# High and low weight parts in alternating places: stationary tiles read with a step of two elements, at eight offsets in turn

## The chip, the cores and the metric

The kernel runs on one core of a Trainium2 chip. Its time is the device time of one execution in microseconds (us); lower is better. Five engines work side by side: PE (matmul; the profile lists its loads of stationary tiles apart, as PEld), DVE (vector), ACT (scalar), POOL, and SP, which issues the DMAs.

## What is computed

One layer of a streaming encoder on 256 tokens of width 2048, all in float32: a mixer of two branches (multi-scale retention and gated DeltaNet), cross-attention to 256 memory tokens, and an MLP of hidden width 8192. Cut to what matters here:

```python
def reference(x, mem, positions, ...):
    h = rms_norm(x, norm_mix_g)
    x = x + hybrid_mixer(h, positions, w_in, conv_w, ..., w_out)   # w_in: 2048 x 18464
    h = rms_norm(x, norm_x_g)
    mem_n = rms_norm(mem, norm_mem_g)
    x = x + cross_attention(h, mem_n, w_xq, w_xkv, w_xo)
    h = rms_norm(x, norm_ffn_g)
    x = x + jnp.square(jax.nn.relu(h @ w_ff1)) @ w_ff2
    return rms_norm(x, norm_final_g)
```

Nearly all of the work is the products of the 256 tokens with the weight matrices, some 390 MB of weights read once.

## The kernel before

A float32 product is made of three products in float32r, a rounded form that PE streams at one pass: every operand is split into a high part (rounded) and a low part (what is left), and high x high, high x low and low x high are added in PSUM.

`fetch` brings a piece of weights to SBUF: one DMA of 1 MB into `raw` (L96), then for each of two halves of 128x1024 a copy on ACT that rounds (L106, writes `whi`) and a subtraction on DVE (L107, writes `wlo`). `whi` and `wlo` are separate tiles with three buffers each, so ACT and DVE run up to three halves ahead of PE. The activations lie in quads: four blocks of 128 features, each with 256 tokens of high parts and 256 of low parts side by side (`both`).

There are two kinds of products:

- `blocks` makes feature-major results (features on the partitions, tokens along them). The weights are the stationary tile, the activations move. For each k-tile and each of two output blocks, L187 multiplies the high weights with the high and the low activations at once (512 columns), L188 the low weights with the high activations (256 columns). One fetch serves 8 k-tiles of two blocks, 16 such pairs. `blocks` makes the delta rule's q, k and v, the retention's q and k, the keys of the cross-attention, w_out, w_xq, w_xo, and the first layer of the MLP. Its evacuation adds the two parts (L194 on ACT, L195 on DVE).
- `chunk` makes token-major results. The activations are the stationary tile, the weights move with 512 columns: L147, L148, L149 for the three products, 16 k-tiles and two token halves to a chunk. It makes the gates, the values and the second layer of the MLP.

The MLP alternates: for each of four parts of the hidden width, a stage of 8 `blocks` (first layer; `evac_h` squares and splits the hidden values into the quads `hid` by L973, L975, L976) and a stage of 4 `chunk`s (second layer).

Where the tiles lie in SBUF: `blocks` puts `whi` 56 elements after the start of its tile and `wlo` at 0 (`AT_BLOCKS`), `chunk` both at 0; pad tiles (`PAD1`, `PAD2`) shift the quads. The order of the instructions on each engine comes from a scheduler that simulates a timeline; fetches have high priority.

Of the kernel before, what the change touches and what calls it, by code (L numbers as in the profile page):

```python
# [11 lines left out]
F32R = mybir.dt.float32r  # L12
# [5 lines left out]
P = 128  # L18
D = 2048
S = 256  # L20
# [10 lines left out]
THETA = 10000.0  # L31


AT_BLOCKS = (56, 0)
PAD1, PAD2 = 8, 80
TWO_PI = 2.0 * math.pi
BIG = 1.0e30
# [14 lines left out]
def trunk(ctx: ExitStack, tc: tile.TileContext, x, mem, positions, norm_mix_g, w_in, conv_w, gdn_a_log, gdn_dt_bias,  # L52
# [8 lines left out]
    wp = ctx.enter_context(tc.tile_pool(name="wpipe", bufs=3))  # L61
    hqp = ctx.enter_context(tc.tile_pool(name="hq", bufs=1))
# [4 lines left out]
    def stream_ps():  # L67
        s0 = psp.tile([P, 512], F32, name="s0", tag="s0", bufs=2)
        s1 = psp.tile([P, 512], F32, name="s1", tag="s1", bufs=2)
        return s0, s1  # L70

    def bank():
        return psp.tile([P, 512], F32, name="b", tag="b", bufs=4)
# [4 lines left out]
    def step():  # L78
        if steps and next(steps[0], steps) is steps:
            steps.pop(0)  # L80
# [3 lines left out]
            step()  # L84


    def fetch(pieces, k, n, rush=False, hold=None, at=(0, 0)):


        raw = wp.tile([P, k * n], F32, name="raw", tag="raw", bufs=3)  # L90
        rv = raw.rearrange("p (k n) -> p k n", k=k)
        with tc.high_priority(offset=100000):
            for off, ap in pieces:
                src = ap.rearrange("(k p) n -> p k n", p=P)
                for ks in ((slice(0, k // 2), slice(k // 2, k)) if rush else (slice(0, k),)):
                    nc.sync.dma_start(rv[:, ks, off:off + ap.shape[1]], src[:, ks, :])  # L96
            got = []
            for i in range(2):
                if hold:
                    both = hold().both  # L100
                    hi, lo = (both[:, a:a + 2, :].rearrange("p a s -> p (a s)") for a in (0, 2))
                else:
                    hi, lo = (wp.tile([P, k * n // 2 + room], F32R, name=nm, tag=nm, bufs=3)[:, a:a + k * n // 2]
                              for nm, a, room in zip(("whi", "wlo"), at, (64, 0)))
                src = raw[:, i * k * n // 2:(i + 1) * k * n // 2]
                act.activation(hi, src, AF.Copy)  # L106
                vec.tensor_sub(lo, src, hi.bitcast(F32))  # L107
                got.append((hi.rearrange("p (k n) -> p k n", n=n), lo.rearrange("p (k n) -> p k n", n=n)))
        return got

    def split(dst, src, at=slice(None)):
        h, l = (a[:, at] for a in dst)
        act.activation(h, src, AF.Copy)
        vec.tensor_sub(l, src, h.bitcast(F32))
# [6 lines left out]
    class Quad(tuple):  # L121
        pass

    def new_quad(pl, bufs):
        both = pl.tile([P, 4, 2 * S], F32R, name="q", tag="q", bufs=bufs)
        quad = Quad((both[:, :, 0:S], both[:, :, S:2 * S]))
        quad.both = both
        return quad

    def quad_a():  # L130
        return new_quad(hqp, 5)

    def chunk(quads, pieces_of, evac, before=None, hold=None):


        ps = stream_ps()
        parts = [(t, 0, 512, ps[t]) for t in range(NT)]
        if hold:
            parts[1:] = [(1, 0, 256, ps[1][:, :256]), (1, 256, 512, bank()[:, :256])]
        held = {q: fetch(pieces_of(q), 4, 512, hold=hold) for q in ((2, 3) if hold else ())}  # L140

        def products(q, i, part, halves):
            t, c0, c1, o = part
            xh, xl = (a[:, i, t * P:(t + 1) * P] for a in quads[q])
            wh, wl = (a[:, i % 2, c0:c1] for a in halves[i // 2])
            first, last = q == 0 and i == 0, q == 3 and i == 3
            pe.matmul(o, xh, wh, start=first, stop=False)  # L147
            pe.matmul(o, xh, wl, start=False, stop=False)  # L148
            pe.matmul(o, xl, wh, start=False, stop=last)  # L149

        for q in range(4):
            if q not in held:
                if before:
                    before(q)
                halves = fetch(pieces_of(q), 4, 512, rush=before is not None and q == 0)
                for i in range(4):
                    for part in parts:
                        products(q, i, part, halves)
                    if i % 2:
                        step()  # L160
        for part in parts:
            for q, halves in held.items():
                for i in range(4):
                    products(q, i, part, halves)
            with tc.high_priority(offset=50000):
                evac(part[0], part[3], part[1], part[2])
# [4 lines left out]
    def blocks(quads, w, c0, nb, evac):  # L171

        k = 16 // nb
        ps = stream_ps()
        n = nb * P
        for g in range(KT // k):
            halves = fetch([(0, w[g * k * P:(g + 1) * k * P, c0:c0 + n])], k, n, at=AT_BLOCKS)
            for i in range(k):  # L180
                kk = g * k + i
                xh, xhl = quads[kk // 4][0][:, kk % 4, :], quads[kk // 4].both[:, kk % 4, :]
                wh, wl = halves[i // (k // 2)]
                for b in range(nb):
                    bs = slice(b * P, (b + 1) * P)
                    lh, ll = wh[:, i % (k // 2), bs], wl[:, i % (k // 2), bs]
                    pe.matmul(ps[b], lh, xhl, start=kk == 0, stop=False)  # L187
                    pe.matmul(ps[b][:, :S], ll, xh, start=False, stop=kk == KT - 1)  # L188
                if i % (k // 2) == k // 2 - 1:
                    step()  # L190
        for b in range(nb):
            with tc.high_priority(offset=50000):
                o = sm.tile([P, S], F32, name="bo", tag="bo", bufs=2)
                act.activation(o, ps[b][:, S:], AF.Copy)  # L194
                vec.tensor_add(o, o, ps[b][:, :S])  # L195
                evac(b, o)
# [108 lines left out]
    def values(n):  # L305
        vo = kv.tile([P, NT, 512], F32, name="vo", tag="vo", bufs=2)

        def evac_kv(t, ps, c0, c1):
            if not mem_scale:
                for c in range(4):  # L310
                    row_squares(mem_rows[c], ssqm, c)
                mem_scale.append(rms_cols("nm", ssqm))
            act.activation(vo[:, t, :], ps, AF.Copy, scale=mem_scale[0][:, t:t + 1])

        chunk(memq, cols(w_xkv[0], D + n * 512), evac_kv, before=load_mem if n == 0 else None)
        nc.sync.dma_start(vv_d[:, :, n * 512:(n + 1) * 512], vo)

    values(0)
    load_gains(16, (norm_mix_g, norm_x_g, norm_ffn_g))
    h1 = [quad_a() for _ in range(4)]  # L320
    ssq1 = cp.tile([P, NT, 4], F32, name="ssq1")
    xcs = [load_rows(c, x, 0) for c in range(4)]
# [5 lines left out]
    for k2 in range(8):  # L328
# [10 lines left out]
        for f in range(2):  # L339
            k = 2 * k2 + f  # L340
# [160 lines left out]

    values(2)
    blocks(h1, w_in[0], C_GA, 1, decay_rows)
    values(3)
    for h in range(4):
# [213 lines left out]
    def retention(j, yr):  # L719
# [16 lines left out]
        def evac_v(t, ps, c0, c1):  # L736
            split(v, ps, t)

        chunk(h1, cols(w_in[0], C_RV + 512 * j), evac_v)
        gng = mx.tile([P, 512], F32, name="gng", tag="g_sq", bufs=1)  # L740
        nc.sync.dma_start(gng, ret_gn_g[0, 512 * j:512 * j + 512].partition_broadcast(P))
# [70 lines left out]
    def take_back(q):  # L812
        if q:
            back = quad_a()
            act.activation(back[0], kept[q - 1], AF.Copy)
            vec.tensor_sub(back[1], kept[q - 1], back[0].bitcast(F32))
            merged.append(back)

    gate_retention, gate_delta_rule = gates()
    for j in range(5):  # L820
# [3 lines left out]
        if j:  # L824
            if j < 4:
                quad = mx.tile([P, 4, S], F32, name="mg", tag="mg", bufs=3)
                kept.append(quad)
            else:
                finish_steps()
                quad = quad_a()  # L830
# [21 lines left out]
    def quad_b():  # L852
        return new_quad(q2p, 4)
# [49 lines left out]
    for h in range(XH):  # L903
# [31 lines left out]
        quad = quad_a()  # L935
        for d2 in range(2):
            ops = bank()
            ov = ops.rearrange("p (d s) -> p d s", d=2)
            for d in range(2):
                c0 = (2 * d2 + d) * P  # L940
# [24 lines left out]
    for fb in range(4):  # L965
        hid = []
        for b2 in range(8):
            hs = fp.tile([P, 2, S], F32, name="hs", tag="hs", bufs=2)
            if b2 % 2 == 0:
                hid.append(quad_a())  # L970

            def evac_h(b, ps):
                vec.scalar_tensor_tensor(hs[:, b, :], ps, 0.0, ps, op0=ALU.max, op1=ALU.mult)  # L973
                qh, ql = (a[:, b2 % 2 * 2 + b, :] for a in hid[-1])
                act.activation(qh, hs[:, b, :], AF.Copy)  # L975
                vec.tensor_sub(ql, hs[:, b, :], qh.bitcast(F32))  # L976

            blocks(h3, w_ff1[0], fb * D + b2 * 256, 2, evac_h)
        for n in range(4):
# [13 lines left out]
            def evac_last(t, ps, c0, c1):  # L993
# [20 lines left out]
                for c in (0, 3, 1, 2):  # L1014
# [13 lines left out]
                  hold=quad_b if last else None)  # L1028
# [27 lines left out]
```

## Time and profile before

| | us |
|---|---|
| median of 3 runs (2107.12 to 2109.13) | 2108.48 |
| the profiled execution | 2106.88 |
| its span, first to last instruction | 2105.2 |
| PE busy (share of the span) | 2083.3 (99%) |
| PE's loads busy | 1796.9 (85%) |
| DVE busy | 1407.7 (67%) |
| ACT busy | 1091.6 (52%) |

The profile shows one execution. A row of a group names the line, the engine, the operation and the tiles (written <- read; for a matmul the moving operand comes first, then the stationary one), the number of instructions, then busy time and the mean of one in ns, then the idle time of the engine ahead of them and what ended it. Matmuls are pipelined: the duration of one holds a latency, so what one costs in a row of many is the distance of two starts. In a window's row stand, after the stretch and its length, each engine's busy time with its count of instructions, the granted PE clock and the share and rate of the DMA engines.

### The profile page before, as it was taken

Reading aid. Unit: us, or ns where it says so; the run is one execution under the profiler, and the core shown is the slowest. Engines: PE = TensorE matmul, PEld = TensorE weight load, DVE = VectorE, ACT = ScalarE, POOL = GpSimd, SP = SyncE. Lnnn points to the kernel's source line nnn. Section 1 sums busy time; section 2 is a strip of 40 time slices with the busy share of each in tenths; the row PEclk is TensorE's granted clock in tenths of the full one; section 3 lists DMA queues with packets and bytes.
Section 4 is the critical chain, followed back from the end, with each engine's and each line's share of the span. In section 5 each row is a group of like instructions: output and inputs, shape, how many; then the busy total and the mean of one; then the engine's idle time right before and its main releaser. Section 6 shows DMA issues by size and latency. Waiting matters only on the chain.

```text
span 2105.2 us, 28781 instructions
## 1 busy us (share of the span) xinstructions
PE 2083.3 (99%) x11172; PEld 1796.9 (85%) x11172; DVE 1407.7 (67%) x2225; ACT 1091.6 (52%) x1700; POOL 28.7 (1%) x39
## 2 busy tenths in 40 slices
PE   8999999999999999999999999999999999999998
PEld 6878888888888888888888899888888888888887
DVE  6756779678758884878557666766556555645655
ACT  7565564565446454655355555554434434434444
POOL 0000000000000000000000000000000000000000
PEclk9999999999999999999999999999999999999999
DMA  8778655555545555555458654566566556556653
GB/s 298 243 242 258 201 181 193 176 171 182 184 156 193 192 175 166 182 183 190 153 174 256 202 186 155 180 197 186 199 190 191 197 187 197 188 192 198 185 198 140
DMA packets 316010, 405.91 MB, mean 193 GB/s; under 512 B 16593, under 2 KB 224481, under 8 KB 315745
## 3 DMA queue, kind: packets, MB, share of 16 engines
q1 hardware_dynamic: 315872, 404.08, 59.5%
q8 instruction: 87, 1.43, 0.3%
q14 instruction: 51, 0.41, 0.1%
HBM read 390.40 MB, written 13.65 MB: 192 GB/s over the span
## 4 chain that ended last, share of the span: by engine, by line
PE 93%; DMA 3%; ACT 2%; DVE 1%; SPq 1%; issue 0%; ACTq 0%; POOLq 0%; POOL 0%; DVEq 0%
PE s L187 32%; PE s L188 17%; PE s L148 13%; PE s L149 13%; PE s L147 13%; PE b L675 2%; DMA dec_d<-dec_w 1%; ACT whi L106 1%; DVE wlo L107 1%; ACT dec_w L493 1%; PE b L581 1%; DMA xc<-x 1%; PE b L117 0%; DMA xt_d<-xt 0%; PE b L119 0%; PE b L118 0%
## 5 line engine op out<-in xcount | busy, mean ns | idle before, releaser
L107 DVE TENSOR_TENSOR wlo<-raw,whi 128x1024 fp32r<-128x1024 f32 x702 | 858.3, 1223 | 522.0 <-ACT whi L106 516.2
L106 ACT ACTIVATE whi<-raw 128x1024 fp32r<-128x1024 f32 x702 | 742.3, 1059 | 730.9 <-PE s L149 387.0
L187 PE MATMUL s<-q,whi 128*128 128x512 f32 x3088 | 1063.4, 390 | 0.7 <-ACT whi L106 0.4
L188 PE MATMUL s<-q,wlo 128*128 128x256 f32 x3088 | 845.3, 281 | 5.2 <-DVE wlo L107 5.1
L187 PEld LDWEIGHTS s<-q,whi 128*128 128x128 f32 x3088 | 570.8, 188 | 111.5 <-ACT whi L106 1.6
L188 PEld LDWEIGHTS s<-q,wlo 128*128 128x128 f32 x3088 | 579.0, 188 | 20.1 <-DVE wlo L107 8.8
L148 PE MATMUL s<-wlo,q 128*128 128x512 f32 x1264 | 495.6, 392 | 1.0 <-DVE wlo L107 1.0
L149 PE MATMUL s<-whi,q 128*128 128x512 f32 x1264 | 492.4, 390 | 0.0
L147 PE MATMUL s<-whi,q 128*128 128x512 f32 x1264 | 454.1, 391 | 0.0
L148 PEld LDWEIGHTS s<-wlo,q 128*128 128x128 f32 x1264 | 238.0, 188 | 50.1 <-DVE wlo L107 2.5
L147 PEld LDWEIGHTS s<-whi,q 128*128 128x128 f32 x1264 | 237.5, 188 | 49.2 <-ACT q L249 0.4
L149 PEld LDWEIGHTS s<-whi,q 128*128 128x128 f32 x1264 | 237.6, 188 | 48.0
L194 ACT ACTIVATE bo<-s 128x256 f32<-128x256 f32 x193 | 73.1, 379 | 118.8 <-PE s L188 105.9
L195 DVE TENSOR_TENSOR bo<-bo,s 128x256 f32<-128x256 f32 x193 | 80.4, 417 | 44.4 <-ACT bo L194 44.1
L534 DVE SCALAR_TENSOR_TENSOR acc<-bo,cw,acc 128x255 f32<-128x255 f32 (+2 forms) x144 | 66.8, 480 | 1.5
L636 DVE TENSOR_TENSOR pr<-lw,tw 32x31 f32<-32x31 f32 (+15 forms) x124 | 40.4, 325 | 8.4 <-DMA lw<-scr_l 6.5
L638 DVE TENSOR_TENSOR tw<-tw,pr 32x31 f32<-32x31 f32 (+15 forms) x124 | 40.5, 327 | 2.1
L782 ACT ACTIVATE gth<-s 128x512 f32<-128x512 f32 x32 | 18.9, 591 | 22.5 <-PE s L149 18.3
L984 DVE SCALAR_TENSOR_TENSOR res<-s,rstd3q,res 128x512 f32<-128x512 f32 (+1 forms) x32 | 22.3, 735 | 11.8 <-PE s L149 11.8
L973 DVE SCALAR_TENSOR_TENSOR hs<-bo 128x256 f32<-128x256 f32 x64 | 27.0, 422 | 1.1
L976 DVE TENSOR_TENSOR q<-hs,q 128x256 fp32r<-128x256 f32 x64 | 26.8, 419 | 0.8 <-ACT q L975 0.8
L531 ACT ACTIVATE acc<-bo,cw 128x256 f32<-128x256 f32 x48 | 24.1, 503 | 4.5 <-DVE bo L195 4.4
(292 smaller groups left out, 1084.3 us busy)
## 6 DMA issues: line engine op xcount, KB each, us to landing
raw<-w_in SPq DMA_DIRECT2D x144, 1024.0 KB, 5.1
raw<-w_ff SPq DMA_DIRECT2D x128, 1024.0 KB, 5.4
raw<-w_xkv SPq DMA_DIRECT2D x31, 1024.0 KB, 5.9
raw<-w_out SPq DMA_DIRECT2D x16, 1024.0 KB, 5.7
raw<-w_xq SPq DMA_DIRECT2D x16, 1024.0 KB, 6.5
raw<-w_xo SPq DMA_DIRECT2D x16, 1024.0 KB, 5.5
dec_d<-dec_w SPq DMA_DIRECT2D x16, 192.0 KB, 4.0
dec<-dec_d SPq DMA_DIRECT2D x8, 384.0 KB, 3.2
```

What stands on the lines that cost most here:

```text
L106: act.activation(hi, src, AF.Copy)
L107: vec.tensor_sub(lo, src, hi.bitcast(F32))
L147: pe.matmul(o, xh, wh, start=first, stop=False)
L148: pe.matmul(o, xh, wl, start=False, stop=False)
L149: pe.matmul(o, xl, wh, start=False, stop=last)
L187: pe.matmul(ps[b], lh, xhl, start=kk == 0, stop=False)
L188: pe.matmul(ps[b][:, :S], ll, xh, start=False, stop=kk == KT - 1)
L194: act.activation(o, ps[b][:, S:], AF.Copy)
L195: vec.tensor_add(o, o, ps[b][:, :S])
L534: vec.scalar_tensor_tensor(acc[:, d:], ps[:, :S - d], cw[:, j, blk:blk + 1], acc[:, d:], op0=ALU.mult, op1=ALU.add)
L638: vec.tensor_sub(tw[:, j + 1:32, 0:j + 1], tw[:, j + 1:32, 0:j + 1], pv)
L675: pe.matmul(pv[:, i, :], lhs(i), rhs[:, i, :], start=True, stop=True)
```

## The change

The high and the low part of a half of weights now share one tile `w`. For `blocks` (`mixed=True`) they alternate, element by element: high parts at even, low parts at odd places. So a stationary tile of 128 columns is read with a step of two elements (8 bytes), and ACT and DVE write, and DVE reads, with that step. For `chunk` the high parts fill the first half of the tile and the low parts the second, contiguous as before. The hidden values of the MLP (`hid`, the second layer's stationary operand) alternate in the same way; all other quads stay as they were. The place in the tile where the parts begin is no longer fixed: every call of `blocks` or `chunk` takes the next of eight offsets, 0 to 56 elements, in steps of 8 (32 bytes).

```diff
-AT_BLOCKS = (56, 0)
+AT_WEIGHTS = (0, 8, 16, 24, 32, 40, 48, 56)
...
-    def fetch(pieces, k, n, rush=False, hold=None, at=(0, 0)):
+    def fetch(pieces, k, n, rush=False, hold=None, at=0, mixed=False):
...
+            half = k * n // 2
             for i in range(2):
+                src = raw[:, i * half:(i + 1) * half]
...
-                    hi, lo = (wp.tile([P, k * n // 2 + room], F32R, name=nm, tag=nm, bufs=3)[:, a:a + k * n // 2]
-                              for nm, a, room in zip(("whi", "wlo"), at, (64, 0)))
-                src = raw[:, i * k * n // 2:(i + 1) * k * n // 2]
+                    w = wp.tile([P, 2 * half + 64], F32R, name="w", tag="w", bufs=3)[:, at:at + 2 * half]
+                    w = w.rearrange("p (n e) -> p e n" if mixed else "p (e n) -> p e n", e=2)
+                    hi, lo = w[:, 0], w[:, 1]
...
+    def next_at():
+        used.append(0)
+        return AT_WEIGHTS[len(used) % len(AT_WEIGHTS)]
...
+    def sides(both, mixed):
+        return both.rearrange("p f (s e) -> p f e s" if mixed else "p f (e s) -> p f e s", e=2)
+
+    def new_quad(pl, bufs, mixed=False):
         both = pl.tile([P, 4, 2 * S], F32R, name="q", tag="q", bufs=bufs)
-        quad = Quad((both[:, :, 0:S], both[:, :, S:2 * S]))
-        quad.both = both
+        pair = sides(both, mixed)
+        quad = Quad((pair[:, :, 0], pair[:, :, 1]))
+        quad.both, quad.pair = both, pair
         return quad
...
     def chunk(quads, pieces_of, evac, before=None, hold=None):
...
+        at = next_at()
...
-                halves = fetch(pieces_of(q), 4, 512, rush=before is not None and q == 0)
+                halves = fetch(pieces_of(q), 4, 512, rush=before is not None and q == 0, at=at)
...
     def blocks(quads, w, c0, nb, evac):
...
+        at = next_at()
         for g in range(KT // k):
-            halves = fetch([(0, w[g * k * P:(g + 1) * k * P, c0:c0 + n])], k, n, at=AT_BLOCKS)
+            halves = fetch([(0, w[g * k * P:(g + 1) * k * P, c0:c0 + n])], k, n, at=at, mixed=True)
...
-                xh, xhl = quads[kk // 4][0][:, kk % 4, :], quads[kk // 4].both[:, kk % 4, :]
+                xh, xhl = quads[kk // 4][0][:, kk % 4, :], quads[kk // 4].pair[:, kk % 4]
...
-                hid.append(quad_a())
+                hid.append(quad_a(mixed=True))
```

After the change the lines are numbered anew: the copy and the subtraction of `fetch` are L108 and L109 (before L106, L107), the products of `blocks` L202 and L203 (L187, L188), those of `chunk` L161 to L163 (L147 to L149), the writes of the hidden quads L990 and L991 (L975, L976).

More of the change, by code (lines that the diff above doesn't have):

```diff
@@ L109, in fetch @@
         return got
+    used = []
+    def next_at():
+        used.append(0)
+        return AT_WEIGHTS[len(used) % len(AT_WEIGHTS)]
     def split(dst, src, at=slice(None)):
@@ L122, in trunk, with quad_a @@
         pass
-    def new_quad(pl, bufs):
+    def sides(both, mixed):
+        return both.rearrange("p f (s e) -> p f e s" if mixed else "p f (e s) -> p f e s", e=2)
+    def new_quad(pl, bufs, mixed=False):
         both = pl.tile([P, 4, 2 * S], F32R, name="q", tag="q", bufs=bufs)
-        quad = Quad((both[:, :, 0:S], both[:, :, S:2 * S]))
-        quad.both = both
-        return quad
-    def quad_a():
-        return new_quad(hqp, 5)
+        pair = sides(both, mixed)
+        quad = Quad((pair[:, :, 0], pair[:, :, 1]))
+        quad.both, quad.pair = both, pair
+        return quad
+    def quad_a(mixed=False):
+        return new_quad(hqp, 5, mixed)
     def chunk(quads, pieces_of, evac, before=None, hold=None):
```

## The prediction

> **What bounds the kernel now.** I read the page first (engines, chain, costliest groups), then the waits of PE, then single stages by windows, and last the starts of single matmuls in the timeline.
>
> ```profile
> span 2105.2 us, 28781 instructions
> PE 2083.3 (99%) x11172; PEld 1796.9 (85%) x11172; DVE 1407.7 (67%) x2225; ACT 1091.6 (52%) x1700; POOL 28.7 (1%) x39
> ...
> PEclk9999999999999999999999999999999999999999
> ...
> PE 93%; DMA 3%; ACT 2%; DVE 1%; SPq 1%; issue 0%; ACTq 0%; POOLq 0%; POOL 0%; DVEq 0%
> PE s L187 32%; PE s L188 17%; PE s L148 13%; PE s L149 13%; PE s L147 13%; PE b L675 2%; DMA dec_d<-dec_w 1%; ACT whi L106 1%; DVE wlo L107 1%; ACT dec_w L493 1%; PE b L581 1%; DMA xc<-x 1%; PE b L117 0%; DMA xt_d<-xt 0%; PE b L119 0%; PE b L118 0%
> ```
>
> PE is busy all through, at the full granted clock, and five matmul lines make 88% of the chain. PE busy is not PE at its peak, so the question is how far apart its matmuls start. Does PE wait for anybody?
>
> ```profile
> PE s L188 <- DVE wlo L107: 5.1, 7, 1.6
> PE b L236 <- DMA xc<-mem: 4.6, 1, 4.6
> ...
> PEld s L188 <- DVE wlo L107: 8.8, 10, 2.0
> ```
>
> Hardly: the largest entries are 5.1 us in 2105. So the change can only matter through the time from one matmul's start to the next, or by making somebody late who is in time today. The starts, in a first-layer stage of the MLP (blocks) and, by count, in a second-layer stage (chunk), where the window's row counts one line in three:
>
> ```profile
> 1606.20 0.39 PE L187 MATMUL s<-q,whi 128*128 128x512 f32 x1
> 1606.42 0.28 PE L188 MATMUL s<-q,wlo 128*128 128x256 f32 x1
> 1606.54 0.39 PE L187 MATMUL s<-q,whi 128*128 128x512 f32 x1
> ...
> 1607.92 0.39 PE L187 MATMUL s<-q,whi 128*128 128x512 f32 x1
> ```
> ```profile
> 1570.30:1658.60 88.30, 87.54 (x256) 47.22 (x255) 1.00 0.63 191
> ...
> 1658.60:1745.70 87.10, 49.80 (x128) 24.02 (x128) 1.00 0.58 193
> ```
>
> 256 pairs in 88.30 us are 345 ns a pair: five pairs from 1606.20 to 1607.92 say the same (344), and within a pair about 227 ns go to the 512-wide L187 and 118 to the 256-wide L188. In the chunk 3 x 128 matmuls in 87.10 us are 227 each. Now the same engine with other operands, float32 instead of float32r:
>
> ```profile
> 316.26 0.59 PE L748 MATMUL b<-qk 128*128 128x256 f32 x2
> 316.69 0.39 PE L749 MATMUL b<-qk 128*128 128x128 f32 x2
> ...
> 385.53 1.05 PE L675 MATMUL b<-r,am 128*128 128x128 f32 x8
> 386.34 0.36 PE L188 MATMUL s<-q,wlo 128*128 128x256 f32 x1
> ```
>
> Two L748 of 256 columns take 0.43 us, 215 each: 0.84 ns a column, half the speed of L187 (227/512 = 0.44). Eight L675 of 128 columns end 1.05 us after the first began; without one 275 ns latency that is 7 steps of 111 ns, and since these stream only 128 columns, 111 is also the most that loading a 128-column stationary tile can cost here. So 215 ns of streaming with a load beside it is possible, and L187 needs 227; a load fits into 111, and L188 needs 118. The surplus is 12 ns on a wide matmul and 7 on a narrow one.
>
> What differs? The load reads 4 bytes per 0.87 ns (111/128). L748's moving operand goes at the same pace, L187's at twice it. Two readers at one pace keep their distance; a reader at twice the pace overtakes the other and can meet it in the same part of the memory. The change makes the load step 8 bytes, so it goes at the pace of a float32r moving operand. That is my main theory: the surplus is paid for these meetings, and a step of two removes most of it.
>
> **The change part by part.**
>
> *Stationary tiles with a step of two.* All L187/L188 loads (3088 each) and those of the second-layer chunks: 4 x 4 chunks x 16 x 2 x 3 = 1536 wide matmuls. The rows are these:
>
> ```profile
> L187 PE MATMUL s<-q,whi 128*128 128x512 f32 x3088 | 1063.4, 390 | 0.7 <-ACT whi L106 0.4
> L188 PE MATMUL s<-q,wlo 128*128 128x256 f32 x3088 | 845.3, 281 | 5.2 <-DVE wlo L107 5.1
> ...
> L148 PE MATMUL s<-wlo,q 128*128 128x512 f32 x1264 | 495.6, 392 | 1.0 <-DVE wlo L107 1.0
> ```
>
> No load with a step of two is in the trace. Best end: 12 x (3088 + 1536) + 7 x 3088 = 77 us less. Worst end: the load takes two of its times, 222 ns; under L187 that is still hidden (227), under L188 it is not, 104 x 3088 = 321 us more. I take the side of L748, with an allowance. At equal pace the distance of the two readers stays what it was at the start, so an offset that collides collides for the whole load. Eight offsets are used in turn; I let two of eight keep today's price and take 1-2 ns off the floor for the rest, 10 and 6 ns gained: 0.75 x (10 x 4624 + 6 x 3088) = 49 us less, all on the path, since PE waits for nothing.
>
> [...]
>
> *The eight offsets under chunks whose stationary tile is contiguous.* 3 x 1264 - 1536 = 2256 matmuls get moving operands at other offsets. Blocks and chunk stand at different offsets today (56 elements, 0) and both show 227. I take nothing, with 3 ns x 2256 = 7 us either way in the range.
>
> *Splitting into alternating places.* The ACT copy and the DVE subtraction now write, and the DVE one also reads, every second element, for 386 of 702 halves (193 block fetches of two).
>
> ```profile
> L107 DVE TENSOR_TENSOR wlo<-raw,whi 128x1024 fp32r<-128x1024 f32 x702 | 858.3, 1223 | 522.0 <-ACT whi L106 516.2
> L106 ACT ACTIVATE whi<-raw 128x1024 fp32r<-128x1024 f32 x702 | 742.3, 1059 | 730.9 <-PE s L149 387.0
> ```
> ```profile
> L638 DVE TENSOR_TENSOR tw<-tw,pr x1: 199/199/199, 311.2 to 311.2; 32x31 f32<-32x31 f32 x1
> ...
> L638 DVE TENSOR_TENSOR tw<-tw,pr x1: 173/173/173, 365.4 to 365.4; 32x31 f32<-32x31 f32 x1
> ...
> L631 DVE MEMSET tw<- x4: 85/85/85, 220.1 to 763.8; 32x32 f32 x4
> ```
>
> The two L638 rows are the same operation on 31 elements: the first jumps 32 elements each time, the last is contiguous. The jumps cost 26 ns, 0.84 ns an element; L631, which writes 32 elements 33 apart, takes 85 ns and shows no such cost. So a strided half costs between 0 and 0.84 x 1024 = 0.86 us more. Does that fit? DVE's busy time by stage (the fifth number), with 10, 33, 18 and 33 halves in it:
>
> ```profile
> 850.00:876.00 26.00, 26.00 (x153) 23.04 (x152) 20.16 (x30) 16.63 (x28) 0.00 (x0) 1.00 0.63 202
> 1106.00:1197.00 91.00, 90.76 (x528) 79.82 (x525) 66.91 (x103) 52.88 (x85) 0.00 (x0) 1.00 0.74 236
> 1350.00:1400.00 50.00, 50.00 (x292) 44.27 (x291) 35.47 (x55) 28.13 (x45) 0.00 (x0) 1.00 0.62 190
> 1570.00:1658.00 88.00, 88.00 (x512) 77.87 (x511) 55.60 (x77) 42.01 (x60) 0.00 (x0) 1.00 0.63 192
> ```
>
> At 0 all is hidden. At 0.86 us: 28.8 of 26, 95.3 of 91, 51.0 of 50, and 84.0 of 88; DVE would be the bound outside the MLP. I take 0, since 8 bytes are far from the 128 of L638. ACT has more room: 42.0 + 28.4 of 88 even at that price. The strided writes of the 64 hidden-layer blocks (256 elements each, at most 0.2 us) are hidden behind the same idle time.
>
> [...]
>
> *One tile for both parts.* In the MLP the order of DVE, and what each instruction waits for, before and after (`w` is the joint tile):
>
> ```order
> L973 SCALAR_TENSOR_TENSOR hs<-bo 128x256 [waits DVE_49]
> L107 TENSOR_TENSOR wlo<-raw,whi 128x1024 [waits PE_49,Activation_49]
> L976 TENSOR_TENSOR q<-hs,q 128x256 [waits Activation_49]
> L107 TENSOR_TENSOR wlo<-raw,whi 128x1024 [waits DMAHW7_49,PE_49,Activation_49]
> L107 TENSOR_TENSOR wlo<-raw,whi 128x1024 [waits PE_49,Activation_49]
> ```
> ```order
> L988 SCALAR_TENSOR_TENSOR hs<-bo 128x256 [waits DVE_49]
> L109 TENSOR_TENSOR w<-raw,w 128x1024 [waits Activation_49]
> L991 TENSOR_TENSOR q<-hs,q 128x256 [waits Activation_49]
> L109 TENSOR_TENSOR w<-raw,w 128x1024 [waits DMAHW7_49,Activation_49]
> L109 TENSOR_TENSOR w<-raw,w 128x1024 [waits Activation_49]
> ```
>
> The subtraction's wait for PE has moved into ACT's copy, which now waits for the last reader of both parts: one L188 later, 0.12 us. Behind it on ACT stand the evacuations (L194), and DVE waits for those.
>
> ```profile
> ACT whi L106 <- PE s L149: 387.0, 245, 4.3
> ACT whi L106 <- PE s L187: 262.7, 209, 2.9
> ```
>
> ACT waits for free buffers already, two halves (2 x 8 x 345 = 5.5 us) ahead of PE, and copy and subtraction need 1.06 + 1.22. A delay of 0.12 us costs nothing. On PE, outside the MLP, the scheduler put the first narrow matmul of some blocks one place later; here a block of w_xkv, before and after:
>
> ```order
> L187 MATMUL s_1457<-q,whi 128x512
> L188 MATMUL s_1457<-q,wlo 128x256
> L187 MATMUL s_1458<-q,whi 128x512
> L188 MATMUL s_1458<-q,wlo 128x256
> ```
> ```order
> L202 MATMUL s_1415<-q,w 128x512
> L202 MATMUL s_1416<-q,w 128x512
> L203 MATMUL s_1415<-q,w 128x256
> L203 MATMUL s_1416<-q,w 128x256
> ```
>
> The same four matmuls, with more time for DVE ahead of the first narrow one: nothing, or a microsecond of the 5.1 us won.
>
> **Sum.** The profiled execution took 2106.9 us by its own clock, 1.6 below the median of 2108.5. 2106.9 - 49 = 2058, and 1.6 more against the median: 2060 us.
>
> **The rivals.**
>
> *More meetings, slower.* A load with a step of two walks over twice the bytes in its time, so it may meet the moving operand twice as often, and there is no proof that L748 is spared for its equal pace: it is also half as fast, so it may simply have slack. Then the surplus doubles: 12 x 4624 + 7 x 3088 = 77 us more, 2186; with a load that is stretched past the 7 ns that L188 has to spare, up to some 2220. It decides from the point where L188's distance passes 118. Against it: two equal paces should part after one collision.
>
> *The load is slower.* 321 us more, 2430, decided when a load passes 118 ns. For it: nothing in the trace, only that no such load has been seen.
>
> *DVE becomes the bound*, outside the MLP, from 0.7 us more a half. Blocks there are (3088 - 1024) x 345 ns = 712 us; overfull by 2 to 11%, 6% in the middle: 43 us more, 2150.
>
> *No change*: the surplus is a fixed cost of changing the stationary tile, equal for any step; 2108. Against it: L748 changes its tile too and has none.
>
> **How the numbers follow.** My forecast, fewer meetings, has 0.45, by itself 2030 (the 77 us end) to 2085. More meetings 0.24, DVE bound 0.13, slow load 0.12, no change 0.05, and 0.01 for something else that is slower. A time within 0.2% is about what a measurement here cannot tell from no change. So faster 0.46 (a hundredth from a partial gain in the other cases), same 0.05, slower 0.49: the likeliest single case is faster, though the slower ones together weigh a little more. The range takes in all but the slow load and the tails: 2030 to 2210.
>
> **What would show it.** Right: in a first-layer stage, pairs 328 to 335 ns apart, and second-layer chunks below 222 a matmul, with offsets visible as groups of blocks. More meetings: pairs above 350 and chunks above 230. Slow load: L203 to L202 above 200 ns, L202 to L203 unchanged. DVE bound: waits of PE for the subtraction in the hundreds of microseconds and L109 near 2 us. The forecast is wrong if pairs stay at 345.

## The result, and the profile after

The changed kernel takes 2146.38 us (median of 4 runs, 2143.98 to 2146.99), the kernel before in the same series 2107.8 us: a ratio of 1.0182 (95% interval 1.0166 to 1.0197), 38.6 us slower. The page of after, its engines, the chain and the groups that answer to those shown of before:

```profile
span 2145.3 us, 28590 instructions
PE 2122.9 (99%) x11172; PEld 1838.9 (86%) x11172; DVE 1409.6 (66%) x2225; ACT 1128.5 (53%) x1700; POOL 28.6 (1%) x39
...
PE 95%; DMA 3%; ACT 1%; DVE 1%; SPq 1%; issue 0%; ACTq 0%; POOLq 0%; POOL 0%; DVEq 0%
...
L109 DVE TENSOR_TENSOR w<-raw,w 128x1024 fp32r<-128x1024 f32 x702 | 859.0, 1224 | 571.7 <-ACT w L108 568.9
L108 ACT ACTIVATE w<-raw 128x1024 fp32r<-128x1024 f32 x702 | 775.9, 1106 | 747.0 <-PE s L163 403.1
...
L202 PEld LDWEIGHTS s<-q,w 128*128 128x128 f32 x3088 | 583.6, 196 | 94.2 <-DVE q L960 0.7
L203 PEld LDWEIGHTS s<-q,w 128*128 128x128 f32 x3088 | 604.7, 196 | 30.9 <-DVE w L109 9.9
```

The same two loads on the page of before:

```profile
L187 PEld LDWEIGHTS s<-q,whi 128*128 128x128 f32 x3088 | 570.8, 188 | 111.5 <-ACT whi L106 1.6
L188 PEld LDWEIGHTS s<-q,wlo 128*128 128x128 f32 x3088 | 579.0, 188 | 20.1 <-DVE wlo L107 8.8
```

PE is still busy for 99% of the span and makes 95% of the chain. The subtraction takes 1224 ns, as before (1223); the copy 1106 on the mean (1059); the record of a load has grown from 188 to 196 ns. The largest wait of PE for the subtraction, in the waits of after:

```profile
PE s L203 <- DVE w L109: 6.0, 8, 1.8
```

That is 6.0 us, where it was 5.1. So no new wait explains the 39 us; the matmuls themselves stand further apart. Windows of after: a first-layer stage (256 pairs, L202 counted) and the second-layer stage before it (3 x 128 matmuls, one line in three counted):

```profile
1777.48:1867.90 90.42, 88.00 (x256) 47.63 (x255) 1.00 0.62 186
...
1687.99:1777.48 89.49, 50.55 (x128) 25.00 (x128) 1.00 0.57 188
```

A pair now takes 353.2 ns (before 344.9), a wide matmul of a chunk 233.0 (before 226.8), at a granted clock of 1.00. The timeline of after shows where in a pair:

```profile
1800.95 0.28 PE L203 MATMUL s<-q,w 128*128 128x256 f32 x1
1801.07 0.40 PE L202 MATMUL s<-q,w 128*128 128x512 f32 x1
1801.31 0.28 PE L203 MATMUL s<-q,w 128*128 128x256 f32 x1
1801.43 0.40 PE L202 MATMUL s<-q,w 128*128 128x512 f32 x1
```

From L203 to L202 it is 0.12 us as before; from L202 to the next L203 it is 0.24, where it was 0.22 to 0.23. Over the whole trace (mean distances of starts, worked out from the timeline) the narrow step stays at 118 ns and the wide one goes from 227 to 233 to 240, by offset. All of the new surplus shows at the wide matmul.

Somewhat under half of the loss lies in the MLP, 18 us: if all four pairs of stages are as long as the one shown, they take 4 x (90.42 + 89.49) = 719.6 us for 4 x (88.30 + 87.10) = 701.6. The other 22 of the 40 us between the two spans lie ahead of it.

### The profile page after: what moved, and what is told of

Read it like the earlier page. It is cut to its first block, busy times and chain, and to the rows that moved or that the text cites. A ratio compares the mean times of both kernels' runs of the same rounds, so it can differ in the third digit from the quotient of the medians.

```text
span 2145.3 us, 28590 instructions
## 1 busy us (share of the span) xinstructions
PE 2122.9 (99%) x11172; PEld 1838.9 (86%) x11172; DVE 1409.6 (66%) x2225; ACT 1128.5 (53%) x1700; POOL 28.6 (1%) x39
## 4 chain that ended last, share of the span: by engine, by line
PE 95%; DMA 3%; ACT 1%; DVE 1%; SPq 1%; issue 0%; ACTq 0%; POOLq 0%; POOL 0%; DVEq 0%
PE s L202 32%; PE s L203 16%; PE s L162 13%; PE s L163 13%; PE s L161 13%; PE b L690 1%; DMA dec_d<-dec_w 1%; ACT dec_w L508 1%; PE b L596 1%; DMA xc<-x 1%; PE b L125 0%; PE b L127 0%; PE b L126 0%; SPq L298 0%; DMA row<-crow 0%; PE b L682 0%
## 5 line engine op out<-in xcount | busy, mean ns | idle before, releaser
L109 DVE TENSOR_TENSOR w<-raw,w 128x1024 fp32r<-128x1024 f32 x702 | 859.0, 1224 | 571.7 <-ACT w L108 568.9
L108 ACT ACTIVATE w<-raw 128x1024 fp32r<-128x1024 f32 x702 | 775.9, 1106 | 747.0 <-PE s L163 403.1
L202 PE MATMUL s<-q,w 128*128 128x512 f32 x3088 | 1074.2, 398 | 0.6 <-DVE q L960 0.5
L203 PE MATMUL s<-q,w 128*128 128x256 f32 x3088 | 822.7, 282 | 6.1 <-DVE w L109 6.0
L202 PEld LDWEIGHTS s<-q,w 128*128 128x128 f32 x3088 | 583.6, 196 | 94.2 <-DVE q L960 0.7
L203 PEld LDWEIGHTS s<-q,w 128*128 128x128 f32 x3088 | 604.7, 196 | 30.9 <-DVE w L109 9.9
L162 PE MATMUL s<-w,q 128*128 128x512 f32 x1264 | 500.9, 396 | 0.6 <-DVE w L109 0.6
L163 PE MATMUL s<-w,q 128*128 128x512 f32 x1264 | 497.9, 395 | 0.0
L161 PE MATMUL s<-w,q 128*128 128x512 f32 x1264 | 458.0, 395 | 0.0
L162 PEld LDWEIGHTS s<-w,q 128*128 128x128 f32 x1264 | 241.7, 191 | 50.6 <-DVE w L109 1.0
L161 PEld LDWEIGHTS s<-w,q 128*128 128x128 f32 x1264 | 240.8, 191 | 51.2 <-ACT q L264 0.4
L163 PEld LDWEIGHTS s<-w,q 128*128 128x128 f32 x1264 | 241.5, 191 | 49.8
L210 DVE TENSOR_TENSOR bo<-bo,s 128x256 f32<-128x256 f32 x193 | 80.3, 416 | 36.1 <-ACT bo L209 36.1
L990 ACT ACTIVATE q<-hs 128x256 fp32r<-128x256 f32 x64 | 27.6, 431 | 0.0
L991 DVE TENSOR_TENSOR q<-hs,q 128x256 fp32r<-128x256 f32 x64 | 26.9, 420 | 0.7 <-ACT q L990 0.7
```

## Experiments

Three suspects stood at the start. The offsets: the places of before were good ones, and what is lost is lost by leaving them, whatever the step. The step: a stationary tile read with a step of two makes its matmuls dearer at any offset. And the joint tile, with the order of the instructions that it changes. "A pair" below is a first-layer stage's length divided by 256, "a wide matmul" a second-layer stage's length divided by 384. Ratios and differences are against the kernel before, run beside: its medians were 2106.46 us for e1 to e4, 2107.21 for e5, e6, e8 and e9, and 2107.52 for the rest.

**e1_offsets_only.** After, with contiguous tiles at the eight offsets:

```diff
-            halves = fetch([...], k, n, at=at, mixed=True)
+            halves = fetch([...], k, n, at=at)
...
-                hid.append(quad_a(mixed=True))
+                hid.append(quad_a())
```

> The change without its step of two: one tile for both parts, eight offsets in turn, but high and low parts contiguous in all weights and quads. Theory A, distance: what a wide matmul costs depends on the distance between the address it streams from and that of the stationary tile that is loaded beside it; before it was 0 (mod 256 bytes) at every wide matmul, 227 ns, and elsewhere it is about 233. Then the first-layer blocks lose as the chunks do: some 5 ns on 3088 + 3700 wide matmuls, 34 us, 2142 us, and a pair of blocks takes about 350 ns. Theory B, step: a load that walks over twice the bytes costs the wide matmul its 8 ns, whatever the offset. Then blocks stay at 345 ns a pair and only the chunks lose, 18 us, 2126 us.

Measured: 2137.46 us, ratio 1.0146 (1.0132 to 1.0159). Windows of this kernel: a first-layer stage; the second-layer stage before it; and of that the second, third and fourth chunk, which stand 56, 0 and 8 elements after the tile's start (96 matmuls each, one line in three counted; the last row ends with the stage, one or two matmuls short):

```profile
1770.85:1860.50 89.65, 87.32 (x256) 45.75 (x255) 1.00 0.62 188
...
1681.87:1770.85 88.98, 50.33 (x128) 24.00 (x128) 1.00 0.58 189
...
1704.73:1727.13 22.40, 12.65 (x33) 6.01 (x32) 1.00 0.56 188
1727.13:1748.91 21.78, 12.45 (x32) 6.01 (x32) 1.00 0.57 193
1748.91:1770.85 21.94, 12.63 (x32) 5.81 (x31) 1.00 0.64 192
```

The offsets alone cost 31 us; of the two expectations the first was near. A pair takes 350.2 ns, a wide matmul 231.7. The chunk at offset 0, the place of before, takes 21.78/96 = 226.9 ns a matmul; the one at offset 56, 224 bytes on and so 32 short of 256, 233.3.

**e2_step_only.** After, with one offset:

```diff
-AT_WEIGHTS = (0, 8, 16, 24, 32, 40, 48, 56)
+AT_WEIGHTS = (0,)
```

> The change without its eight offsets: step of two in the same places, every call at offset 0. The chunks with contiguous stationary tiles are back at distance 0: both theories give them 227 ns. The stationary tiles with a step of two stand at a distance of 0 or 252 bytes. In the changed kernel wide matmuls at these distances took about 234 (blocks) and 233 (second-layer chunks): 6.5 x 3088 + 6 x 1536 = 29 us, 2137 us by both. Against theory A, if the step were harmless at the tuned distance, it would be 2108 us.

Measured: 2144.04 us, ratio 1.0175 (1.0161 to 1.0189). Its windows, first layer and second layer:

```profile
1774.36:1865.03 90.67, 88.17 (x256) 47.62 (x255) 1.00 0.62 186
...
1683.91:1774.36 90.45, 50.98 (x128) 25.14 (x128) 1.00 0.57 186
```

354.2 ns a pair and 235.5 a wide matmul: the step alone costs 38 us, and the second layer more than expected. The offsets alone cost four fifths of the whole and the step alone nearly all of it, so the two don't add up.

**e3_joint_tile.** The joint tile and its order, contiguous, at the places of before:

```diff
-                    w = w.rearrange("p (n e) -> p e n" if mixed else "p (e n) -> p e n", e=2)
-                    hi, lo = w[:, 0], w[:, 1]
+                    hi, lo = w[:, at:at + half], w[:, half + 64:2 * half + 64]
...
-            halves = fetch([...], k, n, at=at, mixed=True)
+            halves = fetch([...], k, n, at=56)
```

> The joint tile alone: high and low parts contiguous in one tile, at the places that the kernel before gave them (56 elements and 0 in blocks, 0 in chunks). Both theories: the kernel before, 2108 us within 0.2%, since ACT, which now waits for the last reader of both parts, is two halves ahead. A third theory, that the joint buffer delays the splitting, gives more, with waits of PE for the subtraction well above 5 us.

Measured: 2108.44 us, ratio 1.0008 (0.9999 to 1.0017). Windows, first layer and second layer, all engines:

```profile
1747.12:1835.66 88.54, 88.54 (x513) 78.18 (x512) 55.60 (x76) 42.65 (x61) 0.00 (x0) 1.00 0.62 190
1660.06:1747.12 87.06, 87.06 (x386) 72.08 (x385) 45.58 (x45) 35.03 (x36) 0.00 (x0) 1.00 0.59 193
```

345.9 and 226.7 ns. The joint tile, its later release and the changed order cost nothing that can be measured. That suspect is out.

**e4_chunk_32 and e5_all_shifted.** Is it the place of a tile, or its distance from another tile? In e4 the chunks' weights alone move by 8 elements; in e5 an unused tile of 8 elements at the start of SBUF moves everything by as much:

```diff
-                halves = fetch(pieces_of(q), 4, 512, rush=before is not None and q == 0)
+                halves = fetch(pieces_of(q), 4, 512, rush=before is not None and q == 0, at=(8, 8))
```
```diff
     cp = ctx.enter_context(tc.tile_pool(name="const", bufs=1))
+    cp.tile([P, 8], F32, name="shift")
```

> The kernel before with the weights of all chunks 8 elements (32 bytes) later in their tiles, everything else at its place and contiguous. Theory A: 3700 wide matmuls go from 227 to about 233 ns, 22 us, 2130 us, and blocks stay at 345 ns a pair. Theory B in its strict form, in which offsets cost little and the step all: 2108 to 2112 us.

> The kernel before with an unused tile of 8 elements at the very start of SBUF, so that every other tile lies 32 bytes later and all distances stay as they were. If the distance between the two operands decides (theory A), this is the kernel before: 2106.5 us within 0.2%, 345 ns a pair, 227 a chunk matmul. If the place of the moving operand itself decides (a start that is 32 past a multiple of 64 bytes), it costs what the 32 bytes cost in the chunks, 6 ns on each of 6800 wide matmuls: 2145 us.

Measured: e4 2128.56 us, ratio 1.0103 (1.0089 to 1.0116); e5 2107.51 us, ratio 1.0003 (0.9994 to 1.0012). Windows of e4, first layer, then second layer:

```profile
1763.51:1851.82 88.31, 87.58 (x256) 47.22 (x255) 1.00 0.63 191
...
1673.92:1763.51 89.59, 50.43 (x128) 23.99 (x128) 1.00 0.57 188
```

Window of e5, second layer:

```profile
1660.23:1747.31 87.08, 49.85 (x128) 24.02 (x128) 1.00 0.60 193
```

e4's chunks go from 226.8 to 233.3 ns a matmul and its blocks stay (345.0); in e5, where the same tiles moved by the same 32 bytes together with the activations, it is 226.8. So it is not the place of the weights as such that counts, but their distance from something that stayed where it was in e4. The row of a matmul names only two tiles that PE reads, the streamed and the stationary one, and in the blocks of e1 it is the stationary one that moved (a pair went from 345 to 350), so the distance between these two is the likeliest. That is argued: every run that moves one of them against the other moves the weights, and `raw` stayed too. The loads in e4 are as busy as before (23.99 us of 128, before 24.02): the matmul is slowed, not the load's record.

**e6_contiguous_scan.** Contiguous tiles as before, 64 pairs of places for the blocks and 16 for the chunks in turn:

```diff
-AT_BLOCKS = (56, 0)
+AT_BLOCKS = [(8 * i, 8 * ((i + j) % 8)) for j in range(8) for i in range(8)]
+AT_CHUNKS = [(4 * i, 4 * i) for i in range(16)]
```

> The kernel before with contiguous tiles, each block at another one of 64 pairs of offsets for high and low parts (0 to 56 elements each), each chunk at one of 16 offsets (0 to 60 elements in steps of 4). Theory A: pairs between 345 and 352 ns, the best at a few pairs of offsets only, among them that of the kernel before (56, 0); chunks 227 at offset 0 and 229 to 235 elsewhere; in all 2130 to 2140 us. If the 227 + 118 are not near the floor, some pairs of offsets go below 340.

Measured: 2132.66 us in one run. Windows, a second-layer stage and the first-layer stage behind it:

```profile
1677.22:1766.32 89.10, 45.38 (x128) 23.92 (x128) 1.00 0.57 189
...
1766.32:1855.99 89.67, 88.93 (x256) 47.26 (x255) 1.00 0.62 188
```

232.0 and 350.3 ns on the mean of the places in these stages. By place (the mean distance of starts, worked out from the timeline): in the second layer a chunk takes 226.7 to 226.8 ns a matmul at distance 0 (counted modulo 256 bytes, a way of counting: no run was made to show the period) and just as little at 240 bytes, then 229.1 at 64 bytes and 231 to 235 at the other places that can be read there; 224 bytes, where the weights stood in e1's slow chunk, takes 233.3 here too. Blocks take 345.0 to 353.3 ns a pair over the 64 combinations, and that of the kernel before (56, 0) 345.5 to 345.9.

The mean of a block hides something, though. The best block, of w_xq with its high parts at 16 elements and its low parts at 0, owes its 345.0 to its first fetch of 16 pairs alone:

```profile
1211.86 0.39 PE L196 MATMUL s<-q,whi 128*128 128x512 f32 x1
1212.08 0.28 PE L197 MATMUL s<-q,wlo 128*128 128x256 f32 x1
1212.20 0.39 PE L196 MATMUL s<-q,whi 128*128 128x512 f32 x1
...
1216.96 0.39 PE L196 MATMUL s<-q,whi 128*128 128x512 f32 x1
```

15 pairs from 1211.86 to 1216.96 are 340 ns each, 227 from the wide matmul to the narrow one and 113 from there to the next; the 16 pairs of the second fetch, at the same offsets, take 350. So the offset within the tile doesn't settle the matter, and a layout better than that of the kernel before does exist for 16 pairs: held for all 3088 it would be worth an estimated (344.9 - 340.0) x 3088 = 15 us. What sets this fetch apart was not followed up.

**e7_step_two_scan.** Is there an offset at which a step of two is cheap? After, with 24 other offsets:

```diff
-AT_WEIGHTS = (0, 8, 16, 24, 32, 40, 48, 56)
+AT_WEIGHTS = tuple(range(2, 64, 4)) + tuple(range(4, 64, 8))
```

> The changed kernel with 24 other offsets in turn, between its eight: multiples of 2 elements (8 bytes). The prediction's idea was that a stepped load and a moving operand run at one pace and keep their distance, so that away from a few colliding distances a pair falls towards 330 ns. If that is so for distances between those tried, some blocks go below 345. If not: 351 to 359 everywhere, 2140 to 2150 us.

Measured: 2148.5 us in one run; a first-layer stage:

```profile
1778.33:1868.51 90.18, 87.77 (x256) 47.52 (x255) 1.00 0.62 187
```

352.3 ns. Worked out by block as above, pairs lie between 350 and 355 ns at these 24 offsets, and between 351 and 359 at the eight of after. None of the 32 comes near 345.

**e8_step_four.** If the load's step costs, a step of four elements should show it plainly. Both halves of a fetch share a tile of four alternating parts (with two buffers of `raw` and of the tile, since it is twice as large); the hidden quads stay contiguous:

```diff
-        raw = wp.tile([P, k * n], F32, name="raw", tag="raw", bufs=3)
+        raw = wp.tile([P, k * n], F32, name="raw", tag="raw", bufs=2)
...
+                w = wp.tile([P, 4 * half + 64], F32R, name="w", tag="w", bufs=2)
+                v = w[:, 0:4 * half].rearrange("p (n e) -> p e n" if apart else "p (e n) -> p e n", e=4)
+                his, los = v[:, 0:2], v[:, 2:4]
```

> Blocks read their weights with a step of four elements: the high and low parts of both halves of a fetch alternate in one tile, two such tiles; to make room, two raw buffers in place of three; hidden quads contiguous, chunks at offset 0. The load's record was 188 ns contiguous and 196 with a step of two. [...] If the step as such is nothing and only the distance counts, pairs stay at 351 to 354 and the time at 2128 to 2140 us.

Measured: 2503.6 us in one run. Its first-layer stage as a window, the groups within that stage, and two pairs of its timeline:

```profile
1867.87:1988.07 120.20, 117.21 (x256) 78.32 (x256) 1.00 0.48 147
```
```profile
L192 PEld LDWEIGHTS s<-q,w 128*128 128x128 f32 x256 | 83.7, 332 | 0.0
L191 PEld LDWEIGHTS s<-q,w 128*128 128x128 f32 x256 | 78.6, 313 | 0.0
...
L111 DVE TENSOR_TENSOR w<-raw,w 128x1024 fp32r<-128x1024 f32 x33 | 64.5, 1998 | 23.2 <-ACT w L110 23.2
...
L110 ACT ACTIVATE w<-raw 128x1024 fp32r<-128x1024 f32 x32 | 61.7, 2033 | 5.9 <-PE s L192 3.4 <-PE s L153 1.5
```
```profile
1900.18 0.51 PE L191 MATMUL s<-q,w 128*128 128x512 f32 x1
...
1900.53 0.28 PE L192 MATMUL s<-q,w 128*128 128x256 f32 x1
...
1900.65 0.51 PE L191 MATMUL s<-q,w 128*128 128x512 f32 x1
```

At a step of four everything that touches the tile takes much longer: a load's record 313 and 332 ns instead of 188, the copy 2033 instead of 1059, the subtraction 1998 instead of 1223. A pair takes 469.5 ns, as two loads in a row at about 235 each would. Yet in the timeline L192 to L191 is 0.12 us and L191 to L192 0.35: if the loads are the bound here, the time that both lose shows at the wide matmul alone, so the starts don't tell which load cost it. A step of two adds 8 ns to the load's record (after), a step of four 125 to 144; why the second adds so much more, no run shows.

**e9_high_parts_only, e10_low_parts_only, e10c_control.** Which of the two loads costs? The high load runs beside the narrow matmul, the low load beside the wide one: in the timeline of after the load of L202 starts with L203, at 1800.95, and that of L203 with L202, at 1801.07. Two theories for it, *path* (P in the expectations) and *interference* (I): by the first only a load that doesn't fit under its matmul costs, so the low one should be free; by the second a stepped load slows the matmul that it runs beside. All three kernels have e8's buffers; in e9 the high parts alone have a step of two, in e10 the low parts alone, in e10c none:

```diff
-                his = w[:, a:a + 2 * half].rearrange("p (n e) -> p e n" if apart else "p (e n) -> p e n", e=2)
-                los = w[:, 2 * half + 64:].rearrange("p (e n) -> p e n", e=2)
+                his = w[:, a:a + 2 * half].rearrange("p (e n) -> p e n", e=2)
+                los = w[:, 2 * half + 64:].rearrange("p (n e) -> p e n" if apart else "p (e n) -> p e n", e=2)
```

> Blocks read their high weights with a step of two (the high parts of both halves alternate), their low weights contiguous, at the offsets of the kernel before (56 and 0); two tiles of four parts and two raw buffers. The load of high weights runs beside the narrow matmul, that of low weights beside the wide one. If a stepped load costs only the wide matmul that runs beside it, nothing changes: 345 ns a pair. If it costs the matmul that uses it, or delays the next load, wide matmuls take about 235 and a pair 352 ns: 2128 us. Fewer buffers may add waits; the pairs' distance tells.

> The twin of the run with stepped high weights: now the low weights have the step of two, the high ones are contiguous, same buffers (two tiles of four parts, two raw buffers), high parts at 56 elements, low at 0. The stepped load runs beside the wide matmul. Theory P, path: the load of the high weights has only a narrow matmul (118 ns) to hide under, so its 8 ns more went onto the path there (351 ns a pair); the load of the low weights has 227 ns and hides: pairs at 345 to 346, 2108 to 2115 us. Theory I, interference: a stepped load takes memory turns from the streaming operand wherever it runs: 348 to 352 a pair.

> The control to both: the same tiles and buffers, high and low weights contiguous at 56 and 0. Pairs at 345 ns, the load's record at 188; in time 2107 us plus what fewer buffers cost (up to 20 us, as waits of PE).

Measured, one run each: e9 2150.2 us, e10 2139.37, e10c 2134.14. The control is 27 us slower than before with nothing stepped, so only the stages are compared. First-layer windows of e9, of e10 and of e10c:

```profile
1779.48:1869.51 90.03, 88.82 (x256) 48.88 (x255) 1.00 0.61 187
```
```profile
1771.51:1860.68 89.17, 87.88 (x256) 46.86 (x255) 1.00 0.62 189
```
```profile
1766.40:1854.83 88.43, 87.29 (x256) 46.76 (x255) 1.00 0.64 190
```

The control's pair takes 345.4 ns; stepped low parts make it 348.3 (+2.9), stepped high parts 351.7 (+6.3). Together that is 9.2, and e2 against e3 gave 8.3 with both. The loads on the pages of e9 (high stepped) and e10 (low stepped):

```profile
L192 PEld LDWEIGHTS s<-q,w 128*128 128x128 f32 x3088 | 596.9, 197 | 125.8 <-ACT w L111 8.5
L193 PEld LDWEIGHTS s<-q,w 128*128 128x128 f32 x3088 | 591.2, 192 | 24.7 <-DVE w L112 12.2
```
```profile
L192 PEld LDWEIGHTS s<-q,w 128*128 128x128 f32 x3088 | 572.6, 189 | 110.1 <-ACT w L111 8.2
L193 PEld LDWEIGHTS s<-q,w 128*128 128x128 f32 x3088 | 600.7, 195 | 25.3 <-DVE w L112 12.5
```

Only the stepped load's record grows much, to 197 and 195. The low load has a whole wide matmul to hide in and still costs 2.9 ns, which speaks against *path*; the high one costs twice as much, as a load would that has 118 ns to fit in and takes 8 more. That last is argued from the sizes and not shown. The starts fit neither theory plainly: in e9, where the stepped load runs beside the narrow matmul, the step from the wide to the narrow start grows from 227 ns (control) to 235, and that from narrow to wide shrinks from 118 to 116; in e10 they are 231 and 117. As in e8, the loss is recorded at the wide matmul whichever load causes it.

**e11_hidden_only.** In the second layer every load stands beside a wide matmul, 226.7 ns from start to start in e3. e3, with the hidden quads alternating:

```diff
-                hid.append(quad_a())
+                hid.append(quad_a(mixed=True))
```

> Only the hidden values of the MLP alternate (the second layer's stationary operand); all weights contiguous in the joint tile at the places of the kernel before. There every load has 227 ns to hide under. Theory P: nothing, 2107 to 2109 us. Theory I: wide matmuls of the second layer go from 227 to 235 as in the step-only run: 7.7 x 1536 = 12 us, 2119 to 2120 us.

Measured: 2118.4 us, ratio 1.0053 (1.0039 to 1.0067). Its second-layer stage:

```profile
1662.52:1752.11 89.59, 50.43 (x128) 24.70 (x128) 1.00 0.56 188
```

233.3 ns a matmul, 6.6 more than in e3, though the load is recorded only 5 ns longer here (24.70 us of 128 are 193 ns, before 188) and could hide. *Interference* holds, *path* falls for the second layer. Where e2 has the same step and the same distances modulo 256 bytes, it took 235.5: the distance so counted doesn't settle the time, and what else does was not found.

## Why the prediction was wrong, point by point

The forecast was 49 us less and a time of 2060; it became 39 us more. The 2146 lie in the range only through the rivals.

*What bounds the kernel.* Right: PE hardly waits before or after (5.1 and 6.0 us in all for the subtraction, the largest entries), and the time changed only through the distance of starts. The time also went where the prediction looked for it, to the step of the wide matmul.

*The reading of L748, on which the sum rested.* This step failed. It took 215 ns of streaming at half pace, without surplus, for proof that two readers of equal pace spare each other. By the prediction's reckoning (a load's element in 0.87 ns, a moving one in 0.44) a step of two gives the load the pace of a float32r moving operand, and nothing was gained by it: where 16 ns less a pair were forecast at most offsets, a pair went from 345.9 (e3) to 354.2 ns (e2), 8.3 more, a wide matmul of the second layer, with only the hidden values stepped, from 226.7 to 233.3 (e11), and no offset of 32 brought a block near 345 (after, e7). In time the step alone took 38 us (e2), where 49 us less were forecast. Of the surplus that the sum wanted to remove, 12 ns of a wide matmul never showed: as the mean of a dozen pairs its step is nowhere below 226 ns in these runs; 5 of the 7 ns of a narrow one went in e6's 16 pairs, with contiguous tiles. The other reading, which stood under the rivals, is not contradicted: L748 streams at 0.84 ns a column where L187 takes 0.44, and may simply have slack. No run tests L748 itself.

*The eight offsets under contiguous tiles.* This term was mis-sized. It was taken as 0, with 7 us either way, because blocks and chunk stood at different offsets and both showed 227 ns. Both had been at good places. Leaving them costs 350.2 - 344.9 = 5.3 ns a pair, 16 us over 3088, and 231.7 - 226.8 = 4.9 ns a wide matmul of the second layer; the 2256 matmuls of which the term spoke lose 11 us at that rate.

*The load's own speed.* The fear of 321 us did not come: the record grew by 8 ns, not by a factor of two. Only a step of four made it two thirds to three quarters longer, 313 and 332 ns for 188 (e8).

*Splitting into alternating places.* Right that it is hidden, and right for DVE, 0 against a bound of 0.86 us. ACT has a price: within a first-layer stage, where all 32 copies alternate, the groups of after show

```profile
L109 DVE TENSOR_TENSOR w<-raw,w 128x1024 fp32r<-128x1024 f32 x32 | 39.3, 1227 | 31.2 <-ACT w L108 31.2
...
L108 ACT ACTIVATE w<-raw 128x1024 fp32r<-128x1024 f32 x32 | 36.5, 1140 | 36.1 <-PE s L203 25.0 <-issue 9.5 <-PE s L163 1.7
```

1140 ns a copy, some 80 more than before's mean, beside 36.1 us of idle time. The subtraction takes 1227 ns a half there, in a first-layer stage of before 1225; at a step of four it took 0.8 us more (1998, e8).

*One tile for both parts, and the order.* Right: nothing (e3).

*The rivals.* "More meetings" came closest: pairs passed 350 and chunks 230, as it asked for. Its size was twice too large (77 us for 39), its deciding point, L188's distance past 118 ns, was not reached, and part of what it saw was the lost places and not the step. "DVE becomes the bound" is out by the 6.0 us of waits: its 0.7 us a half is about what the windows of before leave free outside the MLP, (91.00 - 66.91)/33 = 0.73 in the longest, but no run shows it as the price of a step of two, which cost the subtraction 1 to 2 ns. Out are also "the load is slower" by 353 against some 450 ns a pair, "no change" by the result.

*The new sum.* By the rates of the MLP, blocks give 8.3 x 3088 = 26 us, second-layer chunks 6.2 x 1536 = 10, contiguous chunks 4.9 x 2256 = 11: 47, where 40 lie between the spans. Outside the MLP the loss must be some 7 us less than these rates give; that was not followed up. Nor is it settled why a matmul slows when the tile beside it stands at another distance or is read with a step. The runs show that it does and by how much, and for the chunks that moving everything together changes nothing (e5); distance modulo 256 bytes is not the whole of it (e2 against e11, and the two fetches in e6). The "meetings" are a picture for it, not a finding.

## What to carry to other kernels

Where PE is busy throughout, measure the distance of starts and vary the distance in memory between the streamed and the stationary tile before anything else: 32 bytes under the chunks alone were worth 22 us here, and rotating through eight places gave up the good one seven times in eight (e1). Look at single fetches, not only at means by block: e6's mean of 345 hid 16 pairs at 340. Keep stationary tiles contiguous; a step of two elements cost 2.9 ns a pair (low parts, e10) and 6.6 ns a wide matmul (e11) even where the load seems hidden. An operand without surplus at 0.84 ns a column (L748) told nothing here of one at 0.44 (L187).

## What the runs showed of the hardware that was not expected

- A 512-column float32r matmul with a load beside it took 226.8 ns or 233.3 ns by nothing but a shift of the streamed tiles by 32 bytes (e4), and moving all tiles together changed nothing (e5). A shift by 240 bytes, 16 short of 256, cost nothing either, 226.7 to 226.8 (e6).
- A load with a step of two float32 is recorded 8 ns longer in the blocks (188 to 196, after) and 5 in the second layer (193, e11), and there it slows the wide matmul beside it, in which it could have hidden, by 6.6 ns.
- A step of four float32 makes loads 125 to 144 ns, copies on ACT 0.97 us and subtractions on DVE 0.77 us longer (e8), where a step of two costs DVE nothing and ACT 0.08 us.
- Where both loads of a pair are recorded at 313 and 332 ns, the lost time stands between the starts of the wide matmul and the narrow one (0.35 us, and 0.12 to the next wide one) and not evenly (e8).
